# Two of four heads' normed outputs turned by transposing DMAs through memory, listed behind the next head's softmax

## The chip, the cores and the metric

The kernel runs on one core of a Trainium2 chip. The metric is the device time of one execution in microseconds (us), the median of the runs. The engines are named as in the profile: PE does the matmuls and PEld loads their weights, DVE, ACT and POOL are the vector, scalar and general engines, and SP does nothing but issue DMAs here.

## What is computed

The reference is a trunk of two layers over 256 context and 256 latent tokens of width 1024. Layer 0 mixes tokens with a bidirectional chunkwise mLSTM of four heads, layer 1 with multi-head latent attention, and a gated ConvFFN follows each. What the change touches is the end of layer 0's mixer: each head's output `s` (512 tokens by 512 columns) is gated, normed over the head's columns, and multiplied by the output weights.

```python
def out(h_in, s):
    o = jax.nn.sigmoid(h_in @ w_og).reshape(Bq, T, M_HEADS, M_DV)
    hsum = o * s.transpose(0, 2, 1, 3).astype(h_in.dtype)
    return _head_rms_norm(hsum, norm_g) @ w_out
```

## The kernel before

**Products.** A matmul at full precision is made of three on pairs of a high and a low part: `mm3` (L427) issues high by high (L430), high by low (L433) and low by high (L434). A high part is made by a cast on ACT, a low part by a subtraction on DVE; `split` does both for an activation (L444, L445).

**Weights.** The class Stream brings them in tiles of 128 x 1024 (512 KB), loaded by SP's queue into a ring of three raw buffers (L308), cast by ACT (L345) and subtracted by DVE (L368) into one of three w buffers (some into spare tiles, wu). A w tile serves a step of 24 matmuls. Between them SP loads rows for the modulation vectors (ar, L567), which DVE multiplies and sums (junk, L544). A load is issued when its buffer is free, and SP issues in order.

**The mixer's loop.** For each head h, `w_qk(h)` makes the head's queries and keys in 8 steps of 24 matmuls (192 in all); after a step it advances background work twice (`tick`). Then follow `av(h-1)`, the product of the softmax with the values of the head before (36 matmuls), and `s_mm(h)`, the scores (12 sc and 12 sl), which need all four qk tiles. I call this block h. The background work of block h is `post(h-2)` and then `head(h-1)`. A list in order of background generators is not the order on the engines: a scheduler places each engine's instructions.

- `head` is the softmax of a head: ACT's exponentials (W, L1087), DVE's products and sums over them (L1088 to L1105), and 12 transposes on PE (PT, L1118), split into high and low.
- `av` multiplies by the gate into four tiles of 128 tokens by 512 columns (oh).
- `post` (L1183) norms them: a sum of squares on ACT (jk, L1188), a square root (L1189), a reciprocal and a scaling on DVE (L1192). The next product needs columns in partitions, so 16 transposes of 128 x 128 on PE follow (hnT, L1198), and out of PSUM ACT makes the high part with the norm's gain (hn, L1205) and DVE the low part (L1206), four of each.

The square root and the exponential need different tables on ACT, so a table load stands where the one follows the other.

**After the four blocks.** `outmm("mout")` multiplies hn by the output weights in 16 steps (y), the row of weights k taking hn of row k; head h owns rows 4h to 4h+3. In its first 8 steps the background is `head(3)` and `post(2)`; then comes `av(3)`, and behind it `post(3)`. So hn of heads 0 and 1 is first used at the start of mout.

**Values and gates** of the head before (vr, L1133, and oh) are loaded by POOL's queue in the middle of a block; the softmax's rows (aB) and some pieces of weights (t4d) use that queue too. Tiles of 128 x 512 (S, jk, vr, oh and others) come from a pool called s2 with 15 buffers.

Of the kernel before, what the change touches and what calls it, by code (L numbers as in the profile page):

```python
# [7 lines left out]
F32 = mybir.dt.float32  # L8
F32R = mybir.dt.float32r
I32 = mybir.dt.int32  # L10
AF = mybir.ActivationFunctionType
ALU = mybir.AluOpType
AX = mybir.AxisListType
# [20 lines left out]
NB, NRAW, NU, NS = 3, 3, 31, 15  # L34
# [366 lines left out]
class K:  # L401
# [41 lines left out]
    def split(self, hi, lo, src):  # L443
        self.nc.scalar.copy(hi, src)  # L444
        self.nc.vector.tensor_sub(lo, src, hi)  # L445

    def smc(self, name):
        o, n = self.off[name]
        return self.sm0[:, o:o + n] if o < NSM0 else self.sm[:, o - NSM0:o - NSM0 + n]
# [25 lines left out]
    def setup(self):  # L475
# [3 lines left out]
        self.sm0 = p.tile([128, NSM0], F32, name="sm0")  # L479
        jp = p.tile([128, 128], I32, tag="s2", name="jp", bufs=NS)  # L480
        nc.gpsimd.iota(jp, pattern=[[1, 128]], base=0, channel_multiplier=-1)
# [88 lines left out]
    def ada_all(self, items):  # L570
# [14 lines left out]
        for r in self.bc:  # L585
            nc.scalar.activation(r, r, AF.Silu)  # L586
        yield
# [5 lines left out]
    def mod_tile(self, k):  # L593
# [3 lines left out]
        for g in range(2):  # L597
# [4 lines left out]
            else:  # L602
                nc.scalar.activation(v, v, AF.Identity, bias=sh[:, k, c:c + 1], scale=sc[:, k, c:c + 1])

    def start_up(self):
# [41 lines left out]

        self.tc.keep_in_program_order(nc.scalar.activation(self.tiny(1, "pre"), self.keps, AF.Silu))
        e = mybir.EngineType
# [3 lines left out]
        with self.tc.manual_schedule(engines={e.PE, e.DVE, e.Activation}):  # L653
            for _ in range(WARM):
                nc.tensor.matmul(idle, self.zero[:, 0:128], self.zero, start=True, stop=True)
            for step in STEPS:
                op, n = step[0], [int(x) for x in step[1:]]
                g = n[0]
                if op == "Q":
                    nc.scalar.activation(self.cond[:, :, 0:2], self.smc("cond").rearrange("p (a b) -> p a b", b=2),  # L660
                                         AF.Silu)
                    nc.vector.tensor_scalar(self.ident, self.jp, 0.0, None, op0=ALU.is_equal)
# [24 lines left out]
                elif op == "e":  # L687
# [3 lines left out]
                    nc.vector.tensor_scalar(x[:, c], x[:, c], sc[:, 1:2], sh[:, 1:2], op0=ALU.mult, op1=ALU.add)  # L691
                    nc.scalar.activation(h[:, 0, l], x[:, l], AF.Identity, bias=sh[:, 0:1], scale=sc[:, 0:1])
                    nc.vector.tensor_copy(h[:, 0, c], x[:, c])
# [31 lines left out]
    def conv(self, ps, w3, b, tmp, n):  # L725
        nc = self.nc
        nseg = n // 256
        nc.scalar.activation(tmp[:, :n], ps[:, :n], AF.Identity, bias=b, scale=w3[1])
        t3 = tmp[:, :n].rearrange("p (s t) -> p s t", s=nseg)
# [450 lines left out]
        self.PT = self.vh = self.oh = None  # L1180
        return r

    def post(self, h, tt):  # L1183
        nc = self.nc
        ss = self.tiny(4, "ss")
        jk = self.s2("jk")
        for t in range(4):
            nc.scalar.activation(jk, tt[t], AF.Square, accum_out=ss[:, t:t + 1])  # L1188
        nc.scalar.activation(ss, ss, AF.Sqrt, bias=self.keps, scale=1.0 / 512.0)  # L1189
        nc.vector.reciprocal(ss, ss)  # L1190
        for t in range(4):
            nc.vector.tensor_scalar(tt[t], tt[t], ss[:, t:t + 1], None, op0=ALU.mult)  # L1192
        yield
        g = self.smc("mng")
        for e in range(4):
            pt = self.ps("hnT")
            for t in (2, 0, 1, 3):
                q = nc.tensor.transpose(pt[:, t * 128:(t + 1) * 128], tt[t][:, e * 128:(e + 1) * 128], self.ident)  # L1198
                if e or t != 2:
                    self.behind(q, [lead])  # L1200
                else:
                    lead = q
            k = h * 4 + e
            u = self.u("hn")
            nc.scalar.activation(u[:, 0], pt, AF.Copy, scale=g[:, k:k + 1])  # L1205
            nc.vector.scalar_tensor_tensor(u[:, 1], pt, g[:, k:k + 1], u[:, 0], op0=ALU.mult, op1=ALU.subtract)  # L1206
            self.hn[k] = u
        yield


    def bcast(self, row, name):
        ts = []
        for h in range(2):
            t = self.s2(name)
            self.nc.gpsimd.dma_start(t, row[:, h * 512:(h + 1) * 512].to_broadcast([128, 512]))
            ts.append(t)
        return ts
# [117 lines left out]
    def aout_fin(self, o1, pl, xr, gate, fi, h1u, att):  # L1335
# [86 lines left out]
        def cols(t, pts, n):  # L1422
            mod(t, 0, pts)
            for k in range(0, n, 2):
                mod(t, k + 1, pts)
                split(t, k, 0)
                split(t, k + 1, 0)
                if k + 2 < n:
                    mod(t, k + 2, pts)
                split(t, k, 1)  # L1430
                split(t, k + 1, 1)
# [750 lines left out]
def build(tc, off, a, out):  # L2182
    es = ExitStack()
    with es:
        k = K(tc, es, off, a)
        nc = k.nc
# [12 lines left out]
        k.bg2.append(k.ada_all([(0, 3, 4, 8)] + [(l, c, 0, 8) for l, c in ((0, 4), (0, 5), (1, 0), (1, 1), (1, 2), (1, 3), (1, 4), (1, 5))]))  # L2199
        S = None  # L2200
        tt = None
        k.hn = {}
        for h in range(H0):
            gens = []
            if h == 0:
                gens.append(k.gate_chain())
            if h >= 2:
                gens.append(k.post(h - 2, tt))
            if h >= 1:
                gens.append(k.head(h - 1, S))  # L2210
            k.bg = gens
            k.w_qk(h, 2, (lambda: k.v_load(h - 1)) if h >= 1 else None)
            k.drain()
            if h >= 1:
                tt = k.av(h - 1)
            S = k.s_mm(h)
        k.xc = None
        hn = lambda i: (k.hn[i][:, 0], k.hn[i][:, 1])
        pc = k.acc4()
        k.bg = [k.head(3, S, True), k.post(2, tt)]  # L2220
        vs = k.v_steps(3)
        for i in range(8):
            k.outmm("mout", range(i, i + 1), hn, pc, 0, 16, 2, n2=ADA_M)
            next(vs, None)
        k.drain()
        tt = k.av(3)
        k.bg = [k.post(3, tt)]
        k.outmm("mout", range(8, 12), hn, pc, 0, 16, 1, n2=ADA_M)
        k.drain()
        tokr = a["tok"].rearrange("(t p) d -> t p d", p=128)  # L2230
# [19 lines left out]
        pl = k.acc4()  # L2250
# [70 lines left out]
        pl = k.acc4(True)  # L2321
# [18 lines left out]
        pl = k.acc4(True)  # L2340
# [22 lines left out]
```

## Time and profile before

| | |
|---|---|
| median of the three runs | 1347.13 us (1346.78 to 1347.27) |
| span of the profiled execution | 1345.3 us |
| around the span, against the median | 1.8 us |
| PE busy | 1334.9 us, 99% |
| DVE busy | 1059.0 us, 79% |
| ACT busy | 711.7 us, 53% |
| POOL busy | 141.5 us, 11% |
| block h=3, from its first qk matmul to the first of mout | 517.38 to 576.57 us |

A row of the timeline gives start, duration, engine, line, operation, out<-in and how many; in brackets stands the idle time before it and what ended it. A row of waits gives the engine and line that waited, what released it, and us in total, times and the longest. A matmul's duration in the timeline overlaps the next one's, so the time of one is read from start to start. The chain in order of time gives each piece's start and its own share of the path.

### The profile page before, as it was taken

The numbers are of one execution on the slowest core, as the hardware profiler recorded it, in microseconds if no ns is written. First come the engines' busy times: TensorE is split into PE (matmuls) and PEld (weight loads), VectorE is DVE, ScalarE is ACT, GpSimd is POOL, SyncE is SP. The second block draws the span as 40 slices with busy tenths as digits, with TensorE's granted clock in tenths as the row PEclk, the third lists the DMA queues.
The fourth block names the chain that finished last, engine by engine and source line by source line (L and its number), as shares of the span: only waits on it lengthen the run. The fifth ranks groups of instructions, "written<-read, shape, count | busy, mean of one in ns | idle before, by whom it ended". The sixth has DMA issues, their size and how long they took to land.

```text
span 1345.3 us, 18750 instructions
## 1 busy us (share of the span) xinstructions
PE 1334.9 (99%) x6659; PEld 1120.2 (83%) x6659; DVE 1059.0 (79%) x1745; ACT 711.7 (53%) x1252; POOL 141.5 (11%) x236
## 2 busy tenths in 40 slices
PE   9999999999999999999999999999999999999997
PEld 5777888888888888888898888888888998988886
DVE  4798656678688696897979977758899889898874
ACT  4765444445744546474644334333566767676660
POOL 0222000011101011020002011111000002000100
PEclk9999999999999999999999999999999999999999
DMA  9988848889686384776628989967866437376750
GB/s 364 330 277 279 281 163 248 233 272 307 235 281 230 102 255 149 228 292 222 215 86 261 328 260 286 282 181 184 300 223 194 157 104 219 127 212 189 263 189 32
DMA packets 99885, 304.02 MB, mean 226 GB/s; under 512 B 12312, under 2 KB 25112, under 8 KB 99712
## 3 DMA queue, kind: packets, MB, share of 16 engines
q1 hardware_dynamic: 62992, 218.65, 48.6%
q0 software_dynamic: 26000, 66.75, 17.9%
q10 hardware_dynamic: 10800, 17.44, 3.6%
q8 instruction: 52, 0.85, 0.3%
q14 instruction: 41, 0.34, 0.1%
HBM read 272.21 MB, written 42.12 MB: 234 GB/s over the span
## 4 chain that ended last, share of the span: by engine, by line
PE 97%; DMA 1%; DVE 1%; ACT 0%; issue 0%; SPq 0%; DVEq 0%; ACTq 0%
PE fin L1503 8%; PE tok L430 6%; PE tok L434 6%; PE tok L433 6%; PE fin L433 6%; PE fin L434 6%; PE y L433 6%; PE fin L430 6%; PE y L434 6%; PE y L430 6%; PE qk L430 4%; PE qk L433 4%; PE qk L434 4%; PE up L718 2%; PE up L430 2%; PE up L434 1%
## 5 line engine op out<-in xcount | busy, mean ns | idle before, releaser
L368 DVE TENSOR_TENSOR w<-raw,w 128x1024 fp32r<-128x1024 f32 (+2 forms) x286 | 343.2, 1203 | 131.9 <-ACT w L345 129.7
L345 ACT CAST w<-raw 128x1024 fp32r<-128x1024 f32 (+2 forms) x286 | 296.2, 1037 | 282.4 <-PE tok L434 77.8
L544 DVE SCALAR_TENSOR_TENSOR junk<-ar,bc 128x1024 f32<-128x1024 f32 x128 | 156.1, 1219 | 5.2 <-ACT bc L586 2.3
L433 PE MATMUL fin<-h,w 128*128 128x512 f32 (+1 forms) x370 | 139.6, 377 | 0.0
L430 PE MATMUL fin<-h,w 128*128 128x512 f32 (+1 forms) x370 | 139.5, 377 | 0.0
L434 PE MATMUL fin<-h,w 128*128 128x512 f32 (+1 forms) x370 | 139.3, 377 | 0.0
L1503 PE MATMUL fin<-h,w 128*128 128x512 f32 (+1 forms) x636 | 111.1, 337 | 0.0
L1503 PEld LDWEIGHTS fin<-h,w 128*128 128x128 f32 x636 | 97.6, 190 | 13.2
L430 PE MATMUL qk<-xc,w 128*128 128x512 f32 x256 | 100.2, 391 | 0.0
L434 PE MATMUL qk<-xc,w 128*128 128x512 f32 x256 | 99.8, 390 | 0.0
L433 PE MATMUL qk<-xc,w 128*128 128x512 f32 x256 | 99.6, 389 | 0.0
L433 PEld LDWEIGHTS fin<-h,w 128*128 128x128 f32 x370 | 69.6, 188 | 13.0
L430 PEld LDWEIGHTS fin<-h,w 128*128 128x128 f32 x370 | 69.6, 188 | 12.9
L434 PEld LDWEIGHTS fin<-h,w 128*128 128x128 f32 x370 | 69.6, 188 | 12.6
L434 PEld LDWEIGHTS qk<-xc,w 128*128 128x128 f32 x256 | 48.0, 188 | 10.1
L430 PEld LDWEIGHTS qk<-xc,w 128*128 128x128 f32 x256 | 48.1, 188 | 9.8
L433 PEld LDWEIGHTS qk<-xc,w 128*128 128x128 f32 x256 | 48.1, 188 | 9.8
L430 PE MATMUL tok<-w,hT 128*128 128x512 f32 x128 | 49.9, 390 | 0.0
L433 PE MATMUL tok<-w,hT 128*128 128x512 f32 x128 | 49.8, 389 | 0.0
L434 PE MATMUL tok<-w,hT 128*128 128x512 f32 x128 | 49.8, 389 | 0.0
L735 ACT ACTIVATE fg<-fg 128x512 f32<-128x512 f32 (+1 forms) x44 | 23.1, 525 | 50.0 <-DVE fg L733 43.9
L368 DVE TENSOR_TENSOR wu<-raw,wu 128x1024 fp32r<-128x1024 f32 (+1 forms) x37 | 43.8, 1203 | 3.5 <-ACT wu L345 3.2
(486 smaller groups left out, 3125.7 us busy)
## 6 DMA issues: line engine op xcount, KB each, us to landing
raw<-in_ws SPq DMA_DIRECT2D x282, 512.0 KB, 4.5
ar<-in_adaT SPq DMA_DIRECT2D x80, 512.0 KB, 6.0
t4d<-in_ws POOLq DMA_DIRECT2D x20, 512.0 KB, 9.1
adaw<-in_ada SPq DMA_DIRECT2D x16, 512.0 KB, 8.0
zr<-fd ACTq DMA_DIRECT2D x33, 128.0 KB, 4.6
xmd<-xr POOLq DMA_DIRECT2D x16, 256.0 KB, 4.4
xcd<-cv POOLq DMA_DIRECT2D x16, 256.0 KB, 4.9
xs<-xmd POOLq DMA_DIRECT2D x16, 256.0 KB, 6.0
```

What stands on the lines that cost most here:

```text
L345: self.cast = k.nc.scalar.copy(h[:, :cols], src)
L368: i = self.k.nc.vector.tensor_sub(l[:, :n], src, h[:, :n])
L430: q = mm(out, w[0], x[0], start=start, stop=False, skip_group_check=on)
L433: mm(out, w[0], x[1], start=False, stop=False, skip_group_check=on)
L434: mm(out, w[1], x[0], start=False, stop=stop, skip_group_check=on)
L544: nc.vector.scalar_tensor_tensor(o, w, 1.0, self.bc[j], op0=ALU.mult, op1=ALU.mult, accum_out=col[:, k, j:j + 1])
L718: nc.tensor.matmul(ps[m], wk[i][:, c], hT[k][:, j], start=made[m] == 0, stop=made[m] == 23)
L735: nc.scalar.activation(tmp[:, :n], tmp[:, :n], AF.Silu)
L1503: self.nc.tensor.matmul(ps[:, 0:256] if x else ps, w[x][:, k * 128:(k + 1) * 128], h[:, 0:256] if x else h, start=i == 0 and not k0, stop= ...
```

## The change

For heads 0 and 1, `post` no longer turns its tiles on PE. ACT copies each of the four normed tiles (four-byte numbers) into a tile of two planes of two-byte halves, low halves and high halves apart (`planes`), and POOL's queue writes the four tiles, 256 KB each, to a place in memory (hd). Read as rows of 128 two-byte halves, that place is then loaded by four transposing DMAs on SP's queue, 256 KB each, so that the halves arrive side by side again and each tile (hx) holds 128 columns by 512 tokens. ACT and DVE make the high and low parts of hn from it as before, out of SBUF and not out of PSUM.

A new generator, `mixed`, sets the order of the background in blocks h=2 and h=3: first all of `head(h-1)`, then `post(h-2)`, two empty advances, one transposing load for each of four advances, and then hn in two parts. So the softmax now stands ahead of the norm there; before, the norm came first. Heads 2 and 3 keep PE's transposes (`last=True`).

```diff
+    def planes(self, dst, src):
+
+        i = self.nc.scalar.copy(dst, src.bitcast(U16).rearrange("p (n h) -> p h n", h=2))
+        return i
...
-    def post(self, h, tt):
+    def post(self, h, tt, last=False):
...
         yield
+        if not last:
+            d = self.dr.tile([512, 2, 512], U16, name="hd")
+            for t in range(4):
+                pl = self.pool.tile([128, 2, 512], U16, tag="s2", name="pl", bufs=NS)
+                self.planes(pl, tt[t])
+                nc.gpsimd.dma_start(d[t * 128:(t + 1) * 128], pl)
+            self.turned.append((h, d))
+            yield
+            return
...
+    def mixed(self, head, post):
+
+        nc, g = self.nc, self.smc("mng")
+        yield from head
+        yield from post
+        yield
+        yield
+        h, d = self.turned.pop(0)
+        v = d.rearrange("t h n -> (t h) n")
+        xs = []
+        for e in range(4):
+            x = self.s2("hx")
+            nc.sync.dma_start_transpose(x.bitcast(U16), v[:, e * 128:(e + 1) * 128])
+            xs.append(x)
+            x = None
+            yield
+        for e in range(4):
+            k, x = h * 4 + e, xs[e]
+            u = self.u("hn")
+            nc.scalar.activation(u[:, 0], x, AF.Copy, scale=g[:, k:k + 1])
+            nc.vector.scalar_tensor_tensor(u[:, 1], x, g[:, k:k + 1], u[:, 0], op0=ALU.mult, op1=ALU.subtract)
+            self.hn[k] = u
+            xs[e] = x = None
+            if e % 2:
+                yield
...
             if h >= 2:
-                gens.append(k.post(h - 2, tt))
-            if h >= 1:
+                gens.append(k.mixed(k.head(h - 1, S), k.post(h - 2, tt)))
+            elif h >= 1:
                 gens.append(k.head(h - 1, S))
...
-        k.bg = [k.head(3, S, True), k.post(2, tt)]
+        k.bg = [k.head(3, S, True), k.post(2, tt, True)]
...
-        k.bg = [k.post(3, tt)]
+        k.bg = [k.post(3, tt, True)]
```

On PE the 32 transposes of hnT in the blocks h=2 and h=3 are gone from the order, and the 12 PT of these blocks stand as 4 and 8. The lines of the changed kernel are 1 to 15 higher than those of before. Here is ACT's order at the end of block h=3 before, from the last qk cast but one to the first copy of scores:

```order
L444 CAST qk<-qk 128x512
L444 CAST v<-vr 128x512 x4
L345 CAST w<-raw 128x1024
L559 COPY mod_84<-w 1x1
L345 CAST w<-raw 128x1024
L444 CAST qk<-qk 128x512
L345 CAST w<-raw 128x1024
L345 CAST wu<-raw 128x1024
```

And the same place after, with the planes' copies (pl) ahead of it:

```order
L445 CAST qk<-qk 128x512
L346 CAST w<-raw 128x1024
L450 COPY pl<-oh 128x1024 x4
L565 COPY mod_84<-w 1x1
L346 CAST w<-raw 128x1024
L565 COPY mod_84<-w 1x1 x2
L445 CAST qk<-qk 128x512
L346 CAST w<-raw 128x1024
L565 COPY mod_84<-w 1x1
L445 CAST v<-vr 128x512 x4
L346 CAST w<-raw 128x1024 x2
L1244 ACTIVATE hn<-hx,sm 128x512 x4
```

The next row of after is the last qk cast: the four hn operations, which need the transposing loads, now stand ahead of it, behind two weight casts; in before the four hn stood at the block's start.

SP's order around the transposing loads of block h=3, after (raw are weights, ar the modulation's rows):

```order
L309 DMA raw<-in_ws 128x1024
L1237 DMA_TRANSPOSE hx<-hd 128x1024 x2
L573 DMA ar<-in_adaT 128x1024
L309 DMA raw<-in_ws 128x1024 x2
L1237 DMA_TRANSPOSE hx<-hd 128x1024 x2
L309 DMA raw<-in_ws 128x1024 x8
```

In before only ar and raw loads alternate there. Four loads that wait for POOL's writes now stand between them, two and two.

PE's order in mout, where head 2 is turned and y of its first row follows, before (av is the softmax of head 3 by its values):

```order
L434 MATMUL y<-w,hn 128x512
L1198 MATMUL hnT<-ident,oh 128x128 x16
L430 MATMUL y<-w,hn 128x512
L433 MATMUL y<-w,hn 128x512
L434 MATMUL y<-w,hn 128x512
L430 MATMUL y<-w,hn 128x512
L433 MATMUL y<-w,hn 128x512
L434 MATMUL y<-w,hn 128x512
L430 MATMUL av<-v,PT 128x512
```

And after:

```order
L435 MATMUL y<-w,hn 128x512
L1213 MATMUL hnT<-ident,oh 128x128 x16
L431 MATMUL y<-w,hn 128x512
L434 MATMUL y<-w,hn 128x512
L431 MATMUL y<-w,hn 128x512
L434 MATMUL y<-w,hn 128x512
L431 MATMUL y<-w,hn 128x512
L434 MATMUL y<-w,hn 128x512
L431 MATMUL y<-w,hn 128x512
L431 MATMUL av<-v,PT 128x512
```

Before, six products of the row ahead of head 2's stand between the transposes and av. After, the seven products behind the transposes are those of head 2's first row, without the low by high ones (L435), which come behind av.

3 lines of the change are left out of this document (2 added, 1 removed).

## The prediction

> **What bounds the kernel now.** I read the page first: the span, the busy time of each engine, and the chain that ended last, by engine.
>
> ```profile
> span 1345.3 us, 18750 instructions
> PE 1334.9 (99%) x6659; PEld 1120.2 (83%) x6659; DVE 1059.0 (79%) x1745; ACT 711.7 (53%) x1252; POOL 141.5 (11%) x236
> PE 97%; DMA 1%; DVE 1%; ACT 0%; issue 0%; SPq 0%; DVEq 0%; ACTq 0%
> ```
>
> PE is busy for 99% of the span and is 97% of the chain. Work taken off PE therefore shortens the span, as long as PE does not begin to wait. The view of waits of PE lists all that it waits for in the whole execution:
>
> ```profile
> PE idle L655 <- DVE adav L497: 1.5, 1, 1.5
> PE adar L509 <- DMA adaw<-in_ada: 0.5, 1, 0.5
> PE up L718 <- DVE hT L693: 0.3, 1, 0.3
> PE y L433 <- DVE w L368: 0.2, 1, 0.2
> ```
>
> It is 2.5 us, and none of it is in the mixer, so the change can remove no wait. It can only take PE work away and add waits. The chain in order of time over the mixer gives the PE work that the change touches (start, us, what):
>
> ```profile
> 465.16 1.94 PE hnT L1198 x16
> 487.55 1.31 PE PT L1118 x12
> ...
> 524.35 1.94 PE hnT L1198 x16
> ...
> 546.74 1.31 PE PT L1118 x12
> 585.12 0.44 PE PT L1118 x4
> ...
> 594.91 0.96 PE PT L1118 x8
> 598.62 1.75 PE hnT L1198 x16
> 615.38 1.75 PE hnT L1198 x16
> ```
>
> Four groups of sixteen turning transposes stand there, one for each head. PT are the softmax's own transposes. The timeline of PE gives the clock of block h=3, in which head 1 is turned:
>
> ```profile
> 517.38 0.39 PE L430 MATMUL qk<-xc,w 128*128 128x512 f32 x1
> ...
> 523.96 0.39 PE L434 MATMUL qk<-xc,w 128*128 128x512 f32 x1
> 524.25 2.03 PE L1198 MATMUL hnT<-ident,oh 128*128 128x128 f32 x16
> ...
> 564.23 0.39 PE L430 MATMUL av<-v,PT 128*128 128x512 f32 x1
> 572.39 0.28 PE L430 MATMUL sc<-qk 128*128 128x256 f32 x1
> ```
>
> From 517.38 to 523.96 there are 29 steps from one matmul to the next, so one takes 6.58 / 29 = 0.227 us, and a step of 24 takes 5.44 us. Below, +x means x us after the block's start.
>
> **The change, part by part.**
>
> *PE work removed.* The order drops both hnT groups of the blocks h=2 and h=3: 2 x 1.94 = 3.88 us.
>
> *PE work split.* In both blocks the softmax's twelve PT transposes become 4 and 8. The kernel has such a split in its last block: 0.44 + 0.96 = 1.40 us against 1.31, so 0.09 more. Twice: 0.18. Net so far -3.70 us.
>
> *PT earlier.* The groups also move up: in before 120 matmuls of the block stand ahead of PT, in after 81 (h=2) and 87 (h=3) ahead of the eight. DVE's part of the softmax in before runs from its second W product to the last W:
>
> ```profile
> 529.13 0.41 DVE L1088 SCALAR_TENSOR_TENSOR W<-W,S 128x256 f32<-128x256 f32 x1
> ...
> 544.01 0.74 DVE L1105 SCALAR_TENSOR_TENSOR W<-W,R 128x512 f32<-128x512 f32 x1
> ```
>
> That is 15.6 us, with four junk operations of 1.2 us; in after three stand there, and in h=3 one PT subtraction: some 15 us. It begins, with head's post out of the way, one table load after the S copies, near +2.5, so the last W is ready at about +17.5 in h=2 and, behind the first PT, +18.5 to +19.4 in h=3. PE asks at 81 x 0.227 + 0.44 = +18.8 and 87 x 0.227 + 0.44 = +20.2. About 1 us in hand in each: no cost, a first place for small waits.
>
> *ACT and DVE.* Four copies (pl) are added for each head. A cast of the same 1024 columns is the nearest row:
>
> ```profile
> 524.29 1.03 ACT L345 CAST w<-raw 128x1024 fp32r<-128x1024 f32 x1
> 525.22 2.42 ACT L1205 ACTIVATE hn<-hnT,sm 128x512 fp32r<-128x512 f32 x4
> ...
> 554.03 2.18 ACT L444 CAST v<-vr 128x512 fp32r<-128x512 f32 x4
> ...
> 564.43 0.59 ACT L444 CAST qk<-qk 128x512 fp32r<-128x512 f32 x1 [4.38 <-PE qk L434]
> ```
>
> That is 4 x 1.03 = 4.1 us a head, between 2.2 (as four 512-column casts) and 8.2 (twice, for the halves that are picked apart). The view of windows for the block:
>
> ```profile
> 515.00:574.00 59.00, 59.00 (x281) 49.21 (x280) 45.85 (x90) 33.83 (x68) 6.41 (x12) 1.00 0.60 192
> ```
>
> PE is 59.00 of 59.00, DVE 45.85, ACT 33.83, the granted clock is 1.00. ACT has 25 us free and takes 4 to 8 us beside PE at no cost. The hn operations stay, 2.42 us on ACT and 2.72 on DVE; they move from +8 to the block's end.
>
> ```profile
> 526.50 2.72 DVE L1206 SCALAR_TENSOR_TENSOR hn<-hnT,sm,hn 128x512 fp32r<-128x512 f32 x4
> ```
>
> *The way through memory.* Each head adds four 256 KB writes on POOL's queue (hd) and four transposing loads of 256 KB on SP's. The page's rows for transfers (size, median us to landing), the slowest 256 KB row from the view of DMA:
>
> ```profile
> raw<-in_ws SPq DMA_DIRECT2D x282, 512.0 KB, 4.5
> ...
> vd<-v POOLq DMA_DIRECT2D x16, 256.0 KB, 6.7
> ...
> vr<-vd POOLq DMA_DIRECT2D x16, 256.0 KB, 4.7
> ...
> fd<-fg POOLq DMA_DIRECT2D x11, 256.0 KB, 3.4
> ...
> t4d<-in_ws POOLq DMA_DIRECT2D x4, 256.0 KB, 11.4
> ```
>
> In block h=3 the copies come behind the second PT group at about +20, with w and qk casts between them, and end near +29. The writes land 4 to 7 us later (vd 6.7, fd 3.4): +33 to +36. SP's queue reaches the first two transposing loads before that and waits there, with ar and raw loads behind it. The last two stand behind a raw load that waits for its buffer until about +37. No trace of before shows a transposing load. At 4.7 to 6.7 us (vr, vd) the last lands at +42 to +44; at 11.4, four at once, at +48.
>
> Who needs them: on ACT the four hn operations stand behind a weight cast that waits for the end of w_qk at about +45, and ahead of a qk cast that s_mm needs. That cast's row of before stands above, at 564.43, which is +47.05; s_mm follows at 572.39 in before, +55.0, and 1.9 us earlier with the transposes gone: +53.1. ACT would do hn from +46.05 to +48.5, the qk cast to +49.0, and DVE both low parts by +50.7. PE has 2.4 us in hand behind that, and the loads land 2 to 4 us before ACT asks. In block h=2 all is about 4 us earlier and the qk cast is not late. So I cost this at zero, with both ends kept: at 11.4 each and all at once it is still hidden but for some 0.4 us; passing one after another they may take about (48.5 - 34.5) / 4 = 3.5 us each, and beyond this PE waits.
>
> What the waiting SP instruction holds up: raw loads. How they stand in the mixer (landing), and SP's own waits there:
>
> ```profile
> DMA to landing us min/median/max: 4.0/6.1/9.2
> ...
> SPq L308 <- DVE w L368: 108.5, 20, 17.7
> ```
>
> SP mostly waits for a buffer to come free (108.5 us in 20 times), not the buffers for SP. The three raw buffers feed a step of 5.44 us each: 16.3 us from a buffer's release to its next cast, less 6.1 for the landing and some 2 for cast and subtraction, so a raw load can be 8 us late before ACT's cast, and with the three cast buffers up to two steps more before PE (estimates). A hold of 3 to 6 us is covered; one of 20 is not. On POOL the four v loads now stand behind the four hd writes; they land at +35 to +39, where ACT's v casts begin at +36.7 in before (554.03) and PE uses v from +45. Covered by 4 us.
>
> *The end of the last softmax.* In the last block (mout) ACT gets one more table load ahead of the softmax, since the table of the exponential is no longer loaded when it begins. The row's cost, and what is on the edge there:
>
> ```profile
> 522.68 1.28 ACT L1087 ACT_TABLE_LOAD   x1
> ```
> ```profile
> 593.91 0.74 DVE L1105 SCALAR_TENSOR_TENSOR W<-W,R 128x512 f32<-128x512 f32 x1
> ```
>
> In before this W is done at 593.91 + 0.74 = 594.65, and PE begins the eight PT at 594.80: nothing in hand. In after, PE has five products more ahead of them (5 x 0.227 = 1.13 us later), and the softmax up to 1.28 us more. I take a wait of 0.3 us (0 to 0.6, for what else DVE does between).
>
> *Head 2's turned output.* In before, 6 y products and 36 av stand between hnT (598.62) and the first use of hn of row 8. In after, that use stands directly behind hnT. ACT must first do a weight cast (1.03), a v cast (0.55) and the first hn (0.6): 2.2 us from the point where PE starts hnT, which takes 1.75. I take 0.45 us (0.2 to 0.7).
>
> The sum: -3.88 + 0.18 + 0.30 + 0.45 = -2.95 us. The profiled span is 1345.3 and the median of the runs 1347.13, 1.8 outside the span that does not change. **1347.13 - 2.95 = 1344.2.**
>
> *A rule against this change.* PE turns a 128x128 block of four-byte values in 1.94 / 16 = 0.12 us. The Trainium skill, "VectorE: DVE Perf Modes", section "The three transpose paths", gives the crossbar 1309 ns for such a block of two-byte values, and says to use TensorE where PSUM will do as its target. By it one transposing load, eight blocks, would be 10.5 us (an estimate from that page), four in series 42, and the sum by it about +52 us; no run here shows it. The other mark is the same skill's "Advanced Engine Details and Errata", section "X-Bar Transpose (TRN2)", by which they run as fast as other transfers. The rival below stands on rows alone.
>
> **The rivals.** *The gain goes to small waits.* Every PT group, the hn of row 8 and the order of ACT were on the edge (PT8 at 594.80 above). The eight PT of h=2 and h=3 have about 1 us in hand. Two or three more waits of 0.5 to 1 us leave -0.5 to -2.6: about 1345.5. For it: the softmax shares ACT with eight new copies. Against it: PE's whole list of waits is 2.5 us in before. 0.24.
>
> *Slower: the transposing loads pass one after another.* They are many small pieces that gather rows from memory, and the queue may pass one load at a time. From 3.5 us each the last lands after ACT has stalled on hn, the qk cast behind it is late, and PE stands before s_mm. At the 6.1 us of a raw load there: +34.5 + 24.4 = +58.9 in block h=3, 10.4 us past +48.5; in h=2, where the writes land near +31 and ACT asks by +46, +55.4, 9.4 late. Together +19.8 - 3.0: 1364. At 11.4 each +31 + 45.6 and +34.5 + 45.6 give 30.6 + 31.6 - 3.0: 1406. At 4.0 each, 1.0 and 2.0 us late, it is even with before. Nothing in the trace decides it; no 256 KB row has more than 11.4, and these move under load from many queues. 0.18.
>
> *The change does not do what it says:* the order shows the 32 transposes gone, so only a PE that gets slower beside the loads would give 1347. 0.03.
>
> **How the numbers follow.** The forecast has 0.55. A measurement of this kernel can tell about 0.2%, 2.7 us, from no change: the bounds are 1344.4 and 1349.8. With both waits of the last block from none to their upper ends the forecast runs from -3.70 to -2.40, 1343.4 to 1344.7; the part above 1344.4 needs both in their upper halves, about 0.10. Faster: 0.55 - 0.10 = 0.45. Within: 0.10 + 0.24 + 0.03 = 0.37. Slower: 0.18. The range goes from 1343.0 (0.4 us for what the rows cannot tell) to 1350.0, which takes in the small waits and the mild end of the slow case and leaves out some 0.17 above and 0.03 below. The forecast's own range is 1343.4 to 1344.7.
>
> **What would show it.** Right: PE's busy time down by 3.5 to 3.9 us, no PE wait above 0.7 us in the mixer, the transposing loads of block h=3 landed by 1.9 us before its last w_qk product, and waits of a few tenths at the last eight PT and at the y behind head 2's hnT. The step on the loads is wrong if ACT's hn waits for hx and PE's first sc product waits for the qk cast behind it, or if raw loads issued behind them land late and w casts wait. Wrong as a whole: PE busy no shorter, or PE waits in the mixer of over 3 us.

## The result and the profile after

| | before | after |
|---|---|---|
| median | 1347.19 us (1346.78 to 1347.27, 4 runs) | 1357.63 us (1357.26 to 1361.02, 4 runs) |
| ratio | | 1.0083 (95% interval 1.0070 to 1.0096) |
| span of the profiled execution | 1345.3 us | 1356.2 us |
| PE busy | 1334.9 us | 1336.8 us |

The changed kernel is slower by 10.4 us; 3 us faster was forecast, and the range ended at 1350.0. The page of after, and PE's whole list of waits:

```profile
span 1356.2 us, 18729 instructions
PE 1336.8 (99%) x6627; PEld 1120.6 (83%) x6627; DVE 1060.2 (78%) x1745; ACT 720.2 (53%) x1260; POOL 146.3 (11%) x244
```
```profile
PE PT L1124 <- DVE W L1111: 4.8, 1, 4.8
PE sc L434 <- DVE qk L446: 3.7, 2, 3.2
PE idle L661 <- DVE adav L503: 1.5, 1, 1.5
PE y L431 <- ACT hn L1220: 0.5, 1, 0.5
PE sc L431 <- ACT qk L445: 0.3, 1, 0.3
PE up L724 <- DVE hT L699: 0.3, 1, 0.3
```

Thirty-two instructions are gone (x6659 to x6627), yet PE is busy for 1.9 us longer, and it has two new waits of size: 3.2 us at the scores (sc) and 4.8 us at the last softmax's transposes (PT). From the timelines of PE, by the start of each stage:

| stretch | before | after | difference |
|---|---|---|---|
| block h=2, first qk to first sc | 458.20 to 513.21 | 458.44 to 511.52 | -1.93 |
| block h=2, first sc to the next qk | 513.21 to 517.38 | 511.52 to 520.73 | +5.04 |
| block h=3, first qk to first y | 517.38 to 576.57 | 520.73 to 579.34 | -0.58 |
| mout, first y to the next stage's first transpose | 576.57 to 648.26 | 579.34 to 659.28 | +8.25 |

That is 10.8 of the 10.9 us. The gain is there, 1.93 us in a block, and is overpaid at two places. SP's timeline at the end of block h=3, and the transposing loads' tile (durations in ns on SP's queue, then us to landing):

```profile
553.83 7.27 SPq L1237 DMA_TRANSPOSE hx<-hd  x2
561.19 0.65 SPq L573 DMA_DIRECT2D ar<-in_adaT  x1
561.95 1.77 SPq L309 DMA_DIRECT2D raw<-in_ws  x2
563.77 7.55 SPq L1237 DMA_TRANSPOSE hx<-hd  x2
571.42 1.95 SPq L309 DMA_DIRECT2D raw<-in_ws  x4
```
```profile
L1237 SPq DMA_TRANSPOSE hx<-hd x8: 1382/4083/5070, 489.5 to 568.0; - x8
...
DMA to landing us min/median/max: 9.3/9.6/10.4
```

In before, a raw load is issued in 0.33 us. A transposing load holds the queue 1.4 to 5.1 us. The view gives the landing of four of the eight, the first pair of each block: 9.3 to 10.4 us. For the other four, ACT's hn began 5.4 to 10.6 us after their issue. The burst of raw loads for mout (rows with L308 are of before, with L309 of after; the last two rows are its sixth load):

```profile
556.26 14.57 SPq L308 DMA_DIRECT2D raw<-in_ws  x8
571.42 1.95 SPq L309 DMA_DIRECT2D raw<-in_ws  x4
567.64 0.33 SPq L308 DMA_DIRECT2D raw<-in_ws  x1
572.98 0.38 SPq L309 DMA_DIRECT2D raw<-in_ws  x1
```

In after, the first two loads of the burst slip in between the pairs (561.95), 2 us later in the block than in before. The third to the fifth start 8 to 10 us later in the block than before, behind the last pair, and the sixth follows them at once. So four raw loads run together from 571.42. The sixth is issued 52.3 us into the block, where before had 50.3, but ACT gets it 8.7 us after its issue in place of 3.7 (its casts at 581.67, below, and at 571.30 in before). ACT's timeline there:

```profile
572.49 0.72 ACT L1244 ACTIVATE hn<-hx,sm 128x512 fp32r<-128x512 f32 x1 [4.36 <-DMA hx<-hd]
...
581.67 1.05 ACT L346 CAST wu<-raw 128x1024 fp32r<-128x1024 f32 x1 [4.90 <-DMA raw<-in_ws]
582.62 0.59 ACT L1043 ACTIVATE S<-sc 128x512 f32<-128x512 f32 x1
```

The first copy of scores (S) stands behind a weight cast that waits 4.90 us for its raw tile, the sixth of the burst. PE had the sc scores done at 576.6, so the last softmax starts 6 us late, and PE waits for it at PT. What follows is seen on PE's timeline and in the view of windows (the last three columns of a window's row are the granted clock, the DMA engines' share and GB/s):

```profile
592.44 1.11 PE L1124 MATMUL PT<-ident,W 128*128 128x128 f32 x4 [4.77 <-DVE W L1111]
593.21 0.78 PE L431 MATMUL y<-wu,hn 128*128 128x512 f32 x1
593.78 0.63 PE L434 MATMUL y<-wu,hn 128*128 128x512 f32 x1
594.21 0.63 PE L435 MATMUL y<-wu,hn 128*128 128x512 f32 x1
```
```profile
510.00:520.00 10.00, 6.80 (x29) 5.73 (x28) 9.80 (x17) 2.52 (x6) 0.00 (x0) 0.83 0.65 198
590.00:600.00 10.00, 7.56 (x25) 6.19 (x26) 9.86 (x34) 9.97 (x25) 0.00 (x0) 0.66 0.44 165
```

Behind both waits the granted clock is low (0.83 and 0.66 over ten us) and matmuls follow each other every 0.43 us in place of 0.227, until 597.6. In block h=2 the score part is 5.04 us longer, of which the wait is 3.2 and the slow matmuls 1.7, read from start to start. In mout it is 4.8 at PT, 0.5 at hn, and 2.4 for the slow matmuls; what is left of the 8.25 is small. So 4.1 us of the loss are not waits at all, and they stand in the page as busy PE.

In block h=2, DVE's timeline shows how a late load reaches the scores:

```profile
508.05 0.75 DVE L1245 SCALAR_TENSOR_TENSOR hn<-hx,sm,hn 128x512 fp32r<-128x512 f32 x1 [6.22 <-ACT hn L1244]
508.99 1.23 DVE L369 TENSOR_TENSOR w<-raw,w 128x1024 fp32r<-128x1024 f32 x1 [0.19 <-ACT w L346]
510.13 0.75 DVE L1245 SCALAR_TENSOR_TENSOR hn<-hx,sm,hn 128x512 fp32r<-128x512 f32 x1
510.80 1.22 DVE L550 SCALAR_TENSOR_TENSOR junk<-ar,bc 128x1024 f32<-128x1024 f32 x1
...
514.61 0.69 DVE L446 TENSOR_TENSOR qk<-qk 128x512 fp32r<-128x512 f32 x1
```

DVE sits idle for 6.22 us before the third hn, and then does in order a weight subtraction, the fourth hn and three junk operations; only behind them stands the qk subtraction that PE waits for. The junk was listed there as filler and became a toll: without its 3.8 us the subtraction would have ended near 511.5, before PE asked for it at 512.0 (an estimate from these rows).

### The profile page after: what moved, and what is told of

Same layout as the page of the kernel before. It is cut to its first block, busy times and chain, and to the rows that moved or that the text cites. A ratio compares the mean times of both kernels' runs of the same rounds, so it can differ in the third digit from the quotient of the medians.

```text
span 1356.2 us, 18729 instructions
## 1 busy us (share of the span) xinstructions
PE 1336.8 (99%) x6627; PEld 1120.6 (83%) x6627; DVE 1060.2 (78%) x1745; ACT 720.2 (53%) x1260; POOL 146.3 (11%) x244
## 4 chain that ended last, share of the span: by engine, by line
PE 60%; DVE 1%; DMA 1%; ACT 0%; issue 0%; DVEq 0%; SPq 0%
PE fin L1543 8%; PE y L431 6%; PE y L434 6%; PE y L435 6%; PE fin L431 6%; PE fin L435 6%; PE fin L434 6%; PE y L1386 1%; PE qk L435 1%; PE qk L431 1%; PE qk L434 1%; DMA raw<-in_ws 1%; PE fin L1479 1%; PE s L2142 1%; PE PT L2163 1%; PE zT L1334 1%
## 5 line engine op out<-in xcount | busy, mean ns | idle before, releaser
L435 PE MATMUL fin<-h,w 128*128 128x512 f32 (+1 forms) x370 | 139.4, 377 | 0.0
L435 PE MATMUL qk<-xc,w 128*128 128x512 f32 x256 | 99.8, 390 | 0.0
L435 PEld LDWEIGHTS fin<-h,w 128*128 128x128 f32 x370 | 69.6, 188 | 12.9
L435 PEld LDWEIGHTS qk<-xc,w 128*128 128x128 f32 x256 | 48.1, 188 | 10.0
L435 PE MATMUL tok<-w,hT 128*128 128x512 f32 x128 | 49.8, 389 | 0.0
## 6 DMA issues: line engine op xcount, KB each, us to landing
raw<-in_ws SPq DMA_DIRECT2D x282, 512.0 KB, 4.6
ar<-in_adaT SPq DMA_DIRECT2D x80, 512.0 KB, 6.1
t4d<-in_ws POOLq DMA_DIRECT2D x20, 512.0 KB, 9.0
adaw<-in_ada SPq DMA_DIRECT2D x16, 512.0 KB, 7.8
```

Source lines behind the costliest of these rows:

```text
L435: mm(out, w[1], x[0], start=False, stop=stop, skip_group_check=on)
```

## The experiments

The theory after the two traces, called A in the first expectations: the transposing loads are slow and hold SP's queue, so that in block h=2 hn is late (the first loss) and for mout raw loads are late (the second loss). Rivals: the new order of softmax and norm makes the waits, or any way through memory does. Ratios are of the runs of each kernel to the runs of before on the same chip.

**Order alone.** The loop calls the softmax and then the norm with PE's transposes:

```diff
-                gens.append(k.mixed(k.head(h - 1, S), k.post(h - 2, tt)))
+                gens.append(k.head(h - 1, S))
+                gens.append(k.post(h - 2, tt, True))
```

> The softmax of head h-1 listed ahead of the norm of head h-2 as in the changed kernel, but the norm's outputs turned by PE's transposes as in before: no copies of planes, no writes to memory, no transposing loads. Theory A (the price is that of the transposing loads: each holds SP's queue 1.4 to 5.1 us and lands after 9.6 us, so that raw weights and hn come late): PE's waits at sc in block h=2 (3.2 us) and at the last softmax's PT (4.8 us) are gone, and the time is 1346.8 to 1348.3 us. Theory B (the new order of the work on ACT makes the waits): both waits stay and the time is 1356 to 1361 us. Theory C (any way through memory costs this, by its traffic and its wait): as A.

1347.77 us (1346.88 to 1348.49); ratio 1.0004 (0.9994 to 1.0014). No wait at sc or PT; 0.5 us at the y behind head 2's hnT, as the prediction had it. The order alone costs nothing that can be told from none.

**Head 0 alone, head 1 alone** (the second with `h == 3`).

```diff
+                if h == 2:
                     gens.append(k.mixed(k.head(h - 1, S), k.post(h - 2, tt)))
+                else:
+                    gens.append(k.post(h - 2, tt, True))
+                    gens.append(k.head(h - 1, S))
```

> Only head 0 by the transposing loads, in block h=2, as in the changed kernel; head 1 by PE, the norm ahead of the softmax, as in before. All theories: block h=2 takes 62.3 us as in the changed kernel (59.2 in before). Theory A: the raw loads of mout are no longer late, so mout's wait of 4.8 us at PT is gone: 1347.2 + 3.1 = 1350.3 us (1349.5 to 1351.0). Theory B and C: the same for block h=2, and mout without its wait, as no such order and no load stands in block h=3. If mout keeps its wait of over 3 us, all three are wrong about where it comes from.

1351.90 us (1349.49 to 1355.21); ratio 1.0037 (1.0020 to 1.0054). The profiled run, at 1355.19 us, has waits of 3.5 and 4.5 us at sc, two of its four loads landing after 16.1 and 16.7 us, and no wait in mout. It is one of the two slowest of five executions, and the kernel is the least steady of these, so the size of these waits is not that of the median.

> Only head 1 by the transposing loads, in block h=3, as in the changed kernel; head 0 by PE, the norm ahead of the softmax, as in before. Theory A: block h=2 is back at 59.2 us, block h=3 gains 0.6 us and mout loses 8.3 us, from loads alone: 1347.2 - 0.6 + 8.3 = 1354.9 us (1353.5 to 1356.0). Theory B: mout loses the same, by the order in block h=3. If the damage of mout needs the delays of block h=2 as well, mout loses under 4 us and the time is below 1351 us.

1349.61 us (1348.45 to 1350.23); ratio 1.0017 (1.0008 to 1.0026). Block h=2 is back, and mout waits 3.0 us at PT. That is less than expected: alone the two heads cost 4.6 and 2.4 us, together 10.4. In the profiled executions each place has its wait only with the loads of its own block, but the two losses do not simply add; why is not shown. The execution profiled here was the fastest of ten.

**Plain loads in place of transposing ones**, everything else as in the changed kernel; the turning is left out, and the planes' copy doesn't pick the halves apart:

```diff
-            nc.sync.dma_start_transpose(x.bitcast(U16), v[:, e * 128:(e + 1) * 128])
+            nc.sync.dma_start(x.bitcast(U16), d[e * 128:(e + 1) * 128].rearrange("t h n -> t (h n)"))
```

> As the changed kernel, but the eight loads back from memory are plain loads of the same 256 KB, not transposing ones (and the planes' copy does not pick the halves apart): the turning is left out, so hn holds unturned numbers; the order, the copies, the writes, the waits for the writes and the reads' size stay. Theory A: each plain load holds SP's queue 0.33 us and lands in 4 to 7 us, both large waits go, and the time is that of the forecast, 1343.5 to 1345.5 us. Theory B (order) and C (traffic and dependence through memory): the waits of 3.2 and 4.8 us stay at over half their size, 1352 to 1358 us.

1349.64 us (1348.24 to 1351.15); ratio 1.0017 (1.0008 to 1.0027). Both theories miss. PE's waits in the profiled run:

```profile
PE PT L1124 <- DVE W L1111: 3.9, 1, 3.9
...
PE sc L434 <- DVE qk L446: 0.8, 1, 0.8
```

The wait at sc is gone with the transposing, but the one at PT is nearly whole. So 8 of the 10.4 us go with the transposing loads. One more thing differs, though: a transposing load needs rows of all four writes, a plain one those of a single write, so in block h=2 the first plain load is issued at 483.91 where the first transposing one was at 489.52. Part of the 8 us may be that. What is left is 2.4 us over before, some 6 us with the 3.7 us of PE work that is saved. The profiled execution was the slowest of ten.

**Copies and writes only** (PE's transposes kept, nothing read back), and **dead loads** on top (the transposing loads issued at their places, nothing reads them), then the dead loads as plain ones, and as transposing ones from ACT's queue:

```diff
+            if not dead:
+                return
...
-            nc.sync.dma_start_transpose(x.bitcast(U16), v[:, e * 128:(e + 1) * 128])
+            nc.scalar.dma_start_transpose(x.bitcast(U16), v[:, e * 128:(e + 1) * 128])
```

> The softmax ahead of the norm and PE's transposes, with the four copies of planes and the four writes to memory of heads 0 and 1 added, and no load back: what is written is not read. Theory A2 (two prices: at the end of block h=3 the added traffic makes the burst of raw loads for mout late, and ACT's casts of them stand ahead of the copies of the scores, so that the last softmax is late; in block h=2 the transposing loads are slow and hn, the qk cast and the scores are late): half the traffic gives part of the first price, PE's wait at the last softmax's PT is 0 to 2 us, and the time is 1347.5 to 1349.5 us. Theory D (only the hold of SP's queue by transposing loads makes the raw loads late, the traffic is nothing): no wait, 1347.3 to 1348.2 us.

1348.00 us (1347.2 to 1348.4); ratio 1.0005 (0.9996 to 1.0014). No wait at PT, which is theory D's side, though the time lies in both expected ranges.

> As the run with copies and writes only, plus the eight transposing loads of the changed kernel at their places, but nothing reads what they bring: hn still comes from PE's transposes. Both theories: the waits at sc in block h=2 go, since no hn waits for a load; PE's wait at the last softmax's PT is 3 to 5 us, with a slow stretch behind it: 1351 to 1355 us. If the wait at PT goes as well, it came from ACT's wait for hx in block h=3 and not from late raw loads, and the time is 1347.5 to 1349.5 us.

1356.84 us (1356.41 to 1357.92); ratio 1.0072 (1.0060 to 1.0085). Loads that nobody reads cost 8.8 us over the writes alone, by PE's wait at PT and the slow matmuls behind it. ACT waits for raw tiles (from 440 to 660 us), and SP's queue shows why:

```profile
PE PT L1124 <- DVE W L1111: 5.8, 1, 5.8
```
```profile
ACT wu L346 <- DMA raw<-in_ws: 11.3, 3, 5.1
```
```profile
554.99 11.15 SPq L1238 DMA_TRANSPOSE hx<-hd  x2
566.23 3.25 SPq L309 DMA_DIRECT2D raw<-in_ws  x5
```

Two loads hold the queue for 11.15 us, and the burst starts at 566.23, where it started at 556.05 with the writes alone. The wait at sc is gone, as no hn waits. This shows the second loss by itself: the loss in mout needs no reader.

> As the run with dead transposing loads (1356.8 us), but the eight dead loads are plain ones of the same 256 KB (and the planes' copy does not pick the halves apart); hn comes from PE. Theory A2 (added traffic at the end of block h=3 makes the raw loads late, whatever its kind): PE's wait at the last softmax's PT is 3 to 5 us as with dead transposing loads, 1351 to 1357 us. Theory D2 (it is the transposing loads' own hold of SP's queue and their slow passing where other traffic runs): plain loads cost little, PE's wait at PT is under 1.5 us and the time is 1347.5 to 1349.5 us.

1350.28 us (1349.5 to 1351.0); ratio 1.0023 (1.0014 to 1.0033), between the two expectations. Against their own runs of before the three kernels are at +0.8, +3.3 and +9.7 us: of the dead loads' price 2.5 us belong to any loads of these bytes and 6.4 to their being transposing, the later issue included (in block h=3 the first plain load is issued 5.1 us behind the first write, the first transposing one 7.1). From 550 to 580 us, with plain loads and with transposing ones:

```profile
550.00:580.00 30.00, 30.00 (x139) 25.09 (x138) 20.74 (x27) 14.30 (x22) 3.74 (x7) 1.00 0.94 339
```
```profile
550.00:580.00 30.00, 30.00 (x140) 25.07 (x139) 17.74 (x24) 9.30 (x15) 4.51 (x9) 1.00 1.05 311
```

The DMA engines are busier (1.05 against 0.94) and move less (311 against 339 GB/s). Yet the raw loads themselves do not land later: from 550 to 600 us their median, of those whose landing the view gives, is 5.9 us with transposing dead loads, 10.1 with plain ones and 7.4 with the writes alone. What is late with transposing loads is the issue.

> As the run with dead transposing loads on SP's queue (1356.8 us), but the same eight dead loads are issued on ACT's queue, so that SP's raw loads have no transposing load ahead of them in their queue; ACT pays the hold. Theory H (the hold of SP's queue makes the raw loads late): ACT's waits for raw fall to the 3 us of before, and what is left is ACT's own hold: 1348 to 1353 us. Theory X (the transposing loads slow every other transfer on the DMA engines while they run): the raw loads land as late as before, ACT waits over 8 us for raw, and the time is 1355 us or more.

1370.21 us (1367.54 to 1371.43); ratio 1.0169 (1.0154 to 1.0185). The loads held ACT for 1.7 to 9.1 us each, and the first of each block landed after 13.6 and 26.9 us. ACT's waits for raw fell to 4.5 us, near theory H, but a raw load took 9.0 us to land, up to 17.3, where 6.0 and 9.4 were seen from SP's queue, which is theory X's side. With ACT itself blocked the time says nothing on either. The landings above speak for the hold of the queue, but how the 6.4 us divide between it, the wait for all four writes and the slower DMA engines stays open.

**Casts behind the copies of the scores.** The stream's casts of mout get the scheduler's order "behind S", in the changed kernel and in the one with head 1 alone, and in one with head 0's loads moved into block h=3 (next experiment):

```diff
+        k.st.behind = [k.sc]
         k.xc = None
...
+        k.st.behind = []
         k.drain()
         tt = k.av(3)
```

> The changed kernel with one thing other: ACT's weight casts of mout are listed behind the copies of the last scores (S), so that late raw loads no longer stand ahead of the start of the last softmax. If the in-order casts on ACT carry the late raw loads into the softmax, PE's wait of 4.8 us at PT and its slow stretch (together some 7.5 us) go, and h=2's wait at sc stays: 1350 to 1352 us. If PE then waits for a weight instead (y for w), the raw loads are late for PE itself and the time stays above 1355 us.

1358.76 us (1356.79 to 1359.7); ratio 1.0086.

> Only head 1 by transposing loads in block h=3 (1349.6 us), with the same casts behind the copies of the scores. If these casts carry the delay, mout's wait of 3.0 us at PT goes, and the time is 1345.5 to 1347.0 us; if not, 1349 us or more.

1355.17 us (1354.85 to 1356.23); ratio 1.0062.

> Both heads by transposing loads: head 0 with its loads at the start of block h=3 (the run of 1344.5 us), head 1 in block h=3 as in the changed kernel, the casts of mout behind the copies of the scores. If each part adds up: 1344.5 less up to 1.9 for head 1's transposes and plus what the late loads still cost, 1342.5 to 1346 us. If head 1's loads cost PE a wait for hn or for a weight, 1347 us or more.

1366.34 us (1365.28 to 1367.83); ratio 1.0143. All three failed as tests. The scheduler, given the rule, moved more than the casts: several now stand behind S but ahead of the softmax's exponentials, the transposes of PT and hnT move together, and PE waits at PT (3.4), at hnT (3.6) and, in the third, 11.6 us for hn of head 0, which I had put behind head 1's loads. That ACT's order carries the late raw tile into the softmax is read from the trace; it isn't shown by a run.

**Head 0 alone, its loads elsewhere.** The copies and writes stay in block h=2, head 1 is turned by PE, and `mixed` is cut in two generators, `issue` (four loads) and `finish` (hn). Behind the next block's softmax, at the start of the next block, and at the old place with only hn moved:

```diff
+                if h == 2:
+                    gens += [k.head(1, S), k.post(0, tt)]
+                else:
+                    gens += [k.post(1, tt, True), k.head(2, S), k.issue(), k.finish()]
...
+                    gens += [k.issue(True), k.post(1, tt, True), k.head(2, S), k.finish()]
...
+                    gens += [k.head(1, S), k.post(0, tt), iter((0, 0)), k.issue()]
+                else:
+                    gens += [k.finish(), k.post(1, tt, True), k.head(2, S)]
```

> Head 0 alone by the transposing loads, a block later: copies and writes in block h=2 as in the changed kernel, the loads in block h=3 behind the softmax of head 2, hn at the end of that block; head 1 by PE, norm first. Theory A2: block h=2 gains 1.9 us and has no wait; the loads fall at +25 to +40 of block h=3, at the edge of the burst of raw loads, so mout loses 0 to 4 us: 1345.5 to 1349.5 us. Theory D: the loads hold SP's queue some 15 us just ahead of the burst, mout loses as in the run with head 1 alone: 1348 to 1350 us.

1345.57 us (1344.88 to 1346.44); ratio 0.9988 (0.9979 to 0.9996). No PE wait in the mixer; theory D had expected 1348 us or more. The loads stand far apart in block h=3, from 524.1 to 545.3, and two of them have a landing in the view:

```profile
L1239 SPq DMA_TRANSPOSE hx<-hd x4: 1169/1212/2341, 524.1 to 545.3; - x4
DMA to landing us min/median/max: 4.6/4.8/4.9
```

Spread out like this, the four hold the queue for 5.9 us in all.

> Head 0 alone by the transposing loads, a block later, with the loads at the start of block h=3, where the DMA engines are a third busy (0.32 to 0.36 in the windows), into spare tiles of the larger pool; hn at the end of that block; head 1 by PE. Theory A2 and D: nothing late is on the path, no wait of PE over 1 us in the mixer: 1347.2 - 1.9 + 0 to 0.7 = 1345.3 to 1346.0 us. If a transposing load costs by itself wherever it stands (for instance by slowing PE or DVE), the time is 1347 us or more.

1344.52 us (1344.05 to 1346.27); ratio 0.9982 (0.9973 to 0.9990). No PE wait in the mixer. Its loads on SP, which the scheduler set at the end of block h=2:

```profile
502.69 7.81 SPq L1239 DMA_TRANSPOSE hx<-hd  x3
510.60 0.64 SPq L309 DMA_DIRECT2D raw<-in_ws  x1
511.29 1.17 SPq L1239 DMA_TRANSPOSE hx<-hd  x1
```

The same instruction that took 4.1 us of the queue (median) in the changed kernel takes 1.17 us here as the last of the four.

> Head 0 alone, its transposing loads in block h=2 at about their place in the changed kernel, but hn made at the start of block h=3's background, not ahead of block h=2's last qk cast; head 1 by PE, norm first. If what costs in block h=2 is that hn stands ahead of a cast that PE needs, the wait at sc goes and the time is near that of the early loads in block h=3: 1344.5 to 1346.5 us. If the scheduler still puts hn ahead of the scores' copies, part of a wait of up to 4 us moves to the softmax of block h=3: 1347 to 1351 us.

1344.62 us (1344.12 to 1346.12); ratio 0.9984 (0.9975 to 0.9993). All four loads in a row hold SP for 12.7 us in block h=2:

```profile
492.06 12.73 SPq L1239 DMA_TRANSPOSE hx<-hd  x4
```

They land after 6.9 to 11.0 us, no better than in the changed kernel, and nothing is lost: hn no longer stands ahead of a qk subtraction, and no raw load is urgent there. This shows the first loss: in block h=2 it was hn's place in the order of ACT and DVE. All three versions beat before and the change; between the last two there is no difference that can be told. These two win 2.4 to 2.7 us where one group of transposes is 1.94. With the early loads block h=2 itself gains 1.91 and block h=3 0.20, and the rest of the profiled difference lies outside these blocks (before had 0.7 us of waits at adar and at y, L433, which this profile lacks).

**Both heads early in their own blocks**, the norm first as in before, and the same with head 0's hn a block later:

```diff
+                gens += [k.post(h - 2, tt), k.issue(True), k.head(h - 1, S), k.finish()]
```

> Both heads by copies, writes and transposing loads, but in the order of before: the norm with its copies first, then the four loads (into spare tiles of the larger pool), then the softmax, and hn at the end of the block. The loads fall at about +15 to +30 of each block, where the DMA engines are a third busy, and hn is asked 15 us after they land. If place and order are the whole price of the changed kernel, no wait of PE over 1 us is left in the mixer and both groups of 16 transposes are won: 1347.0 - 3.9 + 0 to 1.0 = 1343.1 to 1344.1 us. If the loads cost by themselves, or the copies on ACT make the softmax late, 1345 us or more.

1353.31 us (1351.31 to 1354.51); ratio 1.0044 (1.0031 to 1.0057). The expectation failed. The place was quiet in before, but not with the loads in it. SP, ACT's waits and a window of this run:

```profile
536.60 13.63 SPq L1239 DMA_TRANSPOSE hx<-hd  x4
```
```profile
ACT w L346 <- DMA raw<-in_ws: 18.3, 2, 11.2
```
```profile
540.00:550.00 10.00, 10.00 (x46) 8.29 (x45) 9.90 (x33) 7.49 (x21) 2.65 (x5) 1.00 1.19 265
```

Four loads hold the queue for 13.63 us, 3.4 each; ACT waits up to 11.2 us for a raw load that w_qk needs (the second row is from 440 to 660 us), and PE waits twice at PT, 6.7 us in all.

> As the run with both heads early, but hn of head 0 is made at the start of the background of block h=3. The same theory: 1343.1 to 1344.5 us. If hn at the block's end ahead of the last qk cast costs a little even when the loads have landed, this run is faster than the other by that; if hn at the start of block h=3 makes its softmax late, slower.

1348.97 us (1347.2 to 1350.14); ratio 1.0013 (1.0004 to 1.0022). The same, milder. So place and order are not the whole price: four loads in a row take some 9 to 14 us of the queue in which no raw load behind them may be urgent, and of the places tried only the end of block h=2 has such a stretch. Spread over a whole block, as head 0's loads were in the version of 1345.57 us, they cost no PE wait either. Head 1's loads were not spread over mout in this way, so whether it has a place stays open.

## Why the prediction was wrong, point by point

- *PE work removed*, 1.94 a block: right, 1.93 was measured. *PE work split*, 0.09 a block: in after the 4 and 8 PT of block h=3 take 0.44 and 0.87 on the chain, 1.31 as before; the split is free.
- *PT earlier*, 1 us in hand: right, no wait there in blocks h=2 and h=3.
- *ACT's copies*: 3.9 us for four, 4.1 forecast; done at +28.7, +29 forecast. *The writes*: median 4.3 us to landing, right.
- **The step that failed first: what the waiting SP instruction holds up.** The prediction gave raw loads 8 us of slack before ACT's cast, from three buffers of a step each, and reckoned with a hold of 3 to 6 us. In after the four loads had SP's queue from 553.83 to 571.32, 17.5 us with three ordinary loads between. In block h=3 no cast of w_qk waited for a raw load even so; the burst of eight at its end, when loads for spare tiles follow each other, did. Before already had no slack there, in a row that I did not look for. ACT's order of before, shown ahead of the prediction, ends at the first wu cast; three more stand between it and the copy of scores, and one of them is this:

```profile
571.30 1.06 ACT L345 CAST wu<-raw 128x1024 fp32r<-128x1024 f32 x1 [2.98 <-DMA raw<-in_ws]
```

  ACT waited 2.98 us for raw, and the next of its casts ended at 573.54, half a us before the copy of scores at 574.02. The changed kernel started the third to the fifth load of that burst 8 to 10 us later in the block, and the one that ACT waits for landed 7 us later in it. This made the larger part of the loss, most of the +8.25 us in mout. None of the rivals named the place, though the signs of being wrong named late raw loads; the run with dead loads shows it with no hn waiting at all.
- **The step mis-sized: the landing.** The term took 4.7 to 6.7 us from plain rows and no time on the queue. Measured were 9.3 to 10.4 us for the first pair of each block, and 4.1 us of SP each in the median. In block h=3 the last pair was issued at +43 and +47, where +37 was forecast, and block h=2's third hx came at 507.29, +48.9, against a deadline of +46. The rival of loads that pass one after another had the mechanism for block h=2 and the point from which it decides (3.5 to 4 us each) about right (4.1 us was measured), and 18% as its chance; it put the price into both blocks' scores, where block h=3 paid 0.8 us only.
- *The qk cast in block h=2 is not late*: this left out the three junk operations that stand on DVE between hn's low parts and the qk subtraction, 3.8 us more. In block h=3 none stand there; *DVE both low parts by +50.7* came to +54.2, since the last hn waited for its load until +52.6.
- *Small terms in mout*: 0.45 us at head 2's hn was right (0.5 measured, with order alone too). The table load's 0.3 at PT can't be seen under the 4.8; with order alone there is no wait.
- *The rival of small waits*: two or three more waits of 0.5 to 1 us on a forecast of -2.95 leave -1.95 to +0.05, not -0.5 to -2.6.
- *Left out entirely*: what a PE wait costs beyond itself, 4.1 us here.
- *Rule against this change*: the Trainium skill, "VectorE: DVE Perf Modes", section "The three transpose paths", by which a load of eight blocks would take 10.5 us (an estimate from that page). The traces agree with its direction and not with its size: four in a row held the queue for 13.63 us, 3.4 each, a third of that figure. They do not agree with the Trainium skill, "Advanced Engine Details and Errata", section "X-Bar Transpose (TRN2)", by which such loads are as fast as others: dead transposing loads cost 6.4 us more than dead plain ones of the same bytes, and with them busier DMA engines moved 311 GB/s in place of 339.

## What to carry to other kernels

Slack isn't a property of a buffer ring but of a moment: before a queue is given slow work, look up who waits for that queue's next loads at that very place, bursts first. An instruction that waits for memory costs what stands behind it on its engine, filler included, so put the reader of a load late and the load where nothing behind it is urgent; moving one reader (hn of head 0) turned a loss of 4.6 us into a gain of 2.4. And with a saturated PE, a wait of several us brings slow matmuls behind it, here half as much again (1.7 us behind 3.2, 2.4 behind 4.8).

## What the runs showed of the hardware

- A transposing load of 256 KB held its queue for 1.2 to 10.9 us in these runs, a plain one on SP's queue for 0.33 to 1.3 us. The short holds do not mean a quick load: with head 0 alone one held the queue for 1.16 us and landed after 16.7. Among the landings that the views give, 3.6 us is the shortest and 18.2 the longest on SP's queue (both in the version with both heads and the casts behind S), and 26.9 the longest on ACT's.
- PE's matmuls were slow behind every PE wait of 3.9 us or more in these runs: at the waits for PT, four matmuls took about 0.43 us after 3.9 us, ten after 4.8, eleven after 5.8. A wait of 2.0 us had none behind it, and of those from 3.0 to 3.7 us some did and some did not. The Trainium skill, "TensorE: Matmul & The Clock Gate", section "Part 1: The HAM clock gate", gives an idle window of about 3.4 us behind which the clock is halved until PE has been busy for as long; the rows of 0.43 against 0.227 us agree with the halving, while waits of 3.0 and 3.2 us that had slow matmuls behind them are shorter than its window.
- The share of the DMA engines alone hid what the loads did: 1.19 at 265 GB/s from 540 to 550 us with both heads early, 1.05 at 311 with dead transposing loads, 0.94 at 339 with plain ones. Both columns have to be read.
